# Two layers of a hybrid attention backbone: one output projection with shared weights, new orders of the work, and the first modulation in blocks of 256 columns

## The chip, the cores and the metric

The kernel runs on one core of one Trainium2 chip. The metric is the device time of one execution in microseconds (us). Times of one instruction are given in nanoseconds (ns).

## The reference

Two layers work on 512 latent tokens and 256 context tokens, all with 1024 features, in float32. Cut to what matters here, a layer is:

```python
shift, scale, gate = split(silu(c) @ w_mod + b_mod)        # once for c, once for c_ctx
h = rms_norm(x, norm_g) * (1 + scale) + shift              # latent and context tokens
p = h @ w_in                                               # 11424 columns: heads, z, g
ya, yb, yc = mla(p), diff(p), swa(p)                       # three attention branches
for r, y in enumerate((ya, yb, yc)):
    term[r] = sigmoid(g[r]) * ((y * silu(z[r])) @ w_branch[r])
x = x + gate * ((term[0] + term[1] + term[2]) @ w_out)     # and the same for ctx in layer 0
```

Keys and values are those of the context and the latent tokens together. Layer 0 also makes the context's new values, layer 1 only the latent ones. At the end stands one more RMS norm.

## The kernel before, in words

All large products run on TensorE (PE) as three matmuls each: an operand is split into a high and a low part in a narrower format, and high x high, high x low and low x high are added in PSUM. A weight item is 128 x 1024 values (0.5 MB). It is loaded into one of two buffers `ws`, split by ScalarE (ACT) into the high part and by VectorE (DVE) into the low part, in tiles `wh`, and taken by the products of L444, as every other product is. So `wh` in a row means weights, `s` the features `h` or heads, `pt` transposed probabilities, `bk` one of four single banks of PSUM and `wd` one of two double ones.

The order of all instructions on all engines is fixed while the program is built. `Plan` (L128) keeps a planned time for each engine; two streams hand it work. `stream_a` (L1008) runs attention units: scores into `wd` (`s_pieces`), a softmax on DVE and ACT, transposes (L914) and products with the values (`tv_pieces`, L904). Between them `t_chain` (L892) copies the transposed tile to its high part on ACT and subtracts it on DVE for the low part. `stream_b` (L1209) runs the dense items in the order of two tables of names: `SEQ` for the projections of the input (`K0` keys, `V` values, `Q0` queries of the windowed branch, and so on) and `BR` for the branch stage. It lets up to `DEPTH` = 2 items be under way. Which stream comes next is decided by the planned times, so that the tables and the planner's costs (`dma_t`, L334, and numbers such as 300.0 in `score`) set the order on the chip.

The program begins with the modulation of layer 0 (`begin`, L1902). Of the 3072 columns of `w_mod`, those for scale and shift are loaded as four pieces of 1024 x 512 (n = 2 and 3 scale, 0 and 1 shift; eight loads of 0.25 MB each, `mod_load`), multiplied by the two conditioning vectors (`mod_mm`, L580), evicted, and turned into columns by four small matmuls (`mod_fin`, L592). Feature f of the eight blocks of 128 features needs the pieces f // 4 and 2 + f // 4. x comes behind the first piece; ACT squares it, DVE normalises it (L665), PE transposes it (L682), ACT or DVE apply scale and shift (L703), and both engines split the result. `start_w` lets the weight items in after n = 1, the last piece. All loads named here are issued by the SP queue, in order.

At the end of a layer `out_entry` multiplies by `w_out` in column pieces: for the four latent tokens' tiles 512 + 256 + 256 columns, and in layer 0 after that 512 + 512 columns for the two context tiles, with weights loaded and split again. Behind the last column piece each tile gets its residual, is stored to `x1d` and normalised in place; `next_h` then transposes it and makes the features of layer 1. In layer 0 `next_h` stands between the latent and the context part.

Of the kernel before, what the change touches and what calls it, by code (L numbers as in the profile page):

```python
# [29 lines left out]
BR = [['z7 z1 z2 g4 z4 z0 z3 g3 z5 z6 g0 b0 g1 b1 g2 b2 b4 g5 b5 b3 g6 b6 g7 b7', 'z7 z5 z0 z1 z6 z2 z3 g0 z4 g1 g2 g3 b3 b1 g4 b2 b0 b4 g5 g6 b5 g7 b6 b7', 'z7 z2 z6 z3 z1 z5 z4 g0 z0 g2 g1 g3 g4 g5 b1 g6 g7 b0 b3 b2 b4 b5 b6 b7'], ['g0 z4 z3 z0 z5 z7 z2 z1 z6 b0 g1 g5 b1 g2 b2 g3 g4 b3 b4 g6 g7 b6 b5 b7', 'z0 z5 z2 z1 g2 z4 z6 z7 g0 g1 z3 b0 g4 b1 g3 b4 g5 b5 b3 g6 b6 b2 g7 b7', 'z1 z4 z0 z2 z5 g0 z7 z6 g2 z3 g1 g5 g3 g4 g6 g7 b1 b2 b3 b4 b5 b0 b6 b7']]  # L30
# [10 lines left out]
START = 1  # L41
# [3 lines left out]
SEQ = ["K0 V Q0 Q1 c0 c1 c2 cn Q2 cr p0 p1 Q3 p2 p3 z20 Q4 K1 z21 Q5 z22 Q6 z23 Q7 v0 k0 q0 z24 k1 q1 v1 k2 q2 l0 l1 ln lr k3 q3 v2 k4 q4 k5 q5 v3 k6 q6 k7 q7 u0 w0 z10 z11 u1 w1 z12 z13 u2 w2 z14 z15 u3 w3",  # L45
       "K0 V Q0 Q1 c0 c1 c2 cn Q2 cr p0 p1 Q3 p2 p3 z20 Q4 K1 z21 Q5 z22 Q6 z23 Q7 v0 k0 q0 z24 k1 q1 v1 k2 q2 l0 l1 ln lr k3 q3 v2 k4 q4 k5 q5 v3 k6 q6 k7 q7 u0 w0 z10 z11 u1 w1 z12 z13 u2 w2 z14 z15 u3 w3"]
# [189 lines left out]
def hybrid_kernel(tc, x_in, c_in, ctx_in, c_ctx, w_mod, b_mod, norm_g, w_in, q_norm, w_uq, kv_norm, w_ukv,  # L236
# [274 lines left out]
    def setup():  # L511
# [7 lines left out]
        n, t = rows_of(sc, (c_in[0], c_ctx), nc.scalar)  # L519
# [62 lines left out]
    def mod_fin(l, n, pm, rel, t):  # L582

        (ev, re), = yield from tmps(1)
        t = yield from act(t, ev, pm, psum=True)
        rel.t = t
        po = {}
        if n < 4:
            def emit():
                po["p"], po["r"] = bk.take()  # L590
                for f in range(4):
# [3 lines left out]
            pv = po["p"][:, 0:8].rearrange("p (f j) -> p j f", j=2)  # L595
            o = l * NCOL
            f0 = (n % 2) * 4
            bm = cols[:, o + COL_B + n * 4:o + COL_B + n * 4 + 4]
            for j in range(2):
                if n < 2:  # L600
                    t = yield from tt(t, modc[:, l, j, 8 + f0:12 + f0], pv[:, j], bm, ALU.add)
                else:
                    a = modc[:, l, j, f0:f0 + 4]
                    t = yield from stt(t, a, pv[:, j], 1.0, bm, ALU.add, ALU.add)
                    t = yield from tt(t, a, a, cols[:, o + COL_G + f0:o + COL_G + f0 + 4], ALU.mult)
# [15 lines left out]
        mod_done[l][n].t = t  # L621

    mod_done = [[When() for _ in range(6)] for _ in range(2)]
# [10 lines left out]
    def mod_now(n, r):  # L634
        o = {}
        for kt in range(8):
            def emit():
                if kt == 0:
                    o["p"], o["r"] = bk.take()
                mod_mm(o["p"], kt, r[kt][0][:, 0:512])  # L640
            t = yield from P.pe(lambda: max(r[kt][1], sil_t.t, bk.gate() if kt == 0 else 0.0), 262.0, emit)
            free(1, t)
        yield from mod_fin(0, n, o["p"], o["r"], t)
# [27 lines left out]
    def make_h(l, H, XN, xdone, lat, fs):  # L671
# [113 lines left out]
    def score(row, kgroups, maps):  # L785
# [9 lines left out]
        P.tick(0.0 if maps == 1 else 300.0)  # L795
# [1106 lines left out]
    def begin():  # L1902
# [54 lines left out]
```

## Time and profile before

| | us |
|---|---|
| median of 3 runs | 2715.02 (2711.09 to 2715.76) |
| the profiled execution | 2711.5 |
| its span, first to last instruction | 2709.7 |
| PE busy | 2632.3 |
| VectorE (DVE) busy | 1615.4 |
| ScalarE (ACT) busy | 1350.7 |
| GpSimd (POOL) busy | 179.3 |

Busy time is the time in which an engine has an instruction under way; matmuls are pipelined, and their ends are modelled. A timeline row begins with the start and the length in us, then engine, line, operation, output and input, the count of merged instructions, and in brackets the idle time before it and what ended that.

### The profile page before, as it was taken

The page shows a single profiled execution, that of the slowest core. Times are in us where ns is not written, and L with a number is a line of the kernel's source. Part 1 is how long each engine was busy: PE and PEld are TensorE (multiplying, and loading weights), DVE is VectorE, ACT ScalarE, POOL GpSimd, SP SyncE. Part 2 cuts the span into 40 slices and gives each one's busy share as a digit, 9 for nine tenths or more (in the row PEclk, how much of TensorE's full clock was granted, in tenths as well). Part 3 has the DMA queues.
Part 4 walks back from the last instruction along what each step waited for, and adds up shares of the span by engine and source line. Part 5 has one row for each costly group of instructions (what it writes and reads, how often), then busy time and mean ns, then how long its engine had stood idle before and what let it go on. Part 6 is the DMA issues. An engine that isn't in the chain of part 4 may idle for free. (4 is left out here: it accounts for less than half of the span.)

```text
span 2709.7 us, 42486 instructions
## 1 busy us (share of the span) xinstructions
PE 2632.3 (97%) x16551; PEld 2291.5 (85%) x16551; DVE 1615.4 (60%) x3010; ACT 1350.7 (50%) x2685; POOL 179.3 (7%) x371
## 2 busy tenths in 40 slices
PE   7999999999999999999999998999999999999998
PEld 5888898888888888888888887898888788888887
DVE  4677887666676652142424577887667676534435
ACT  5676775545665551121222366777546565422333
POOL 2101111111100000000000011111101100000000
PEclk8999999999999999999999999999999999999999
DMA  7133211111132463442322533312111223443433
GB/s 237 47 96 85 66 43 48 53 51 42 49 85 85 140 201 117 121 133 63 103 69 64 186 97 91 85 51 65 55 50 38 72 75 98 122 140 101 131 94 133
DMA packets 332318, 249.55 MB, mean 92 GB/s; under 512 B 24870, under 2 KB 296324, under 8 KB 332116
## 3 DMA queue, kind: packets, MB, share of 16 engines
q1 hardware_dynamic: 331472, 246.50, 31.2%
q8 instruction: 130, 2.13, 0.3%
q0 software_dynamic: 416, 0.30, 0.1%
q14 instruction: 72, 0.59, 0.1%
q10 hardware_dynamic: 228, 0.03, 0.0%
HBM read 211.37 MB, written 35.41 MB: 91 GB/s over the span
## 5 line engine op out<-in xcount | busy, mean ns | idle before, releaser
L444 PE MATMUL wd<-s,wh 128*128 128x512 f32 (+1 forms) x4392 | 852.2, 355 | 2.0 <-DVE s L330 1.5
L444 PEld LDWEIGHTS wd<-s,wh 128*128 128x128 f32 x4392 | 723.7, 189 | 123.1 <-issue 6.7
L444 PE MATMUL bk<-s,wh 128*128 128x512 f32 (+1 forms) x3666 | 763.4, 355 | 8.0 <-DVE s L323 1.8
L444 PEld LDWEIGHTS bk<-s,wh 128*128 128x128 f32 x3666 | 584.2, 190 | 94.9 <-issue 6.8
L323 DVE TENSOR_TENSOR wh<-ws,wh 128x1024 fp32r<-128x1024 f32 (+4 forms) x294 | 324.3, 1108 | 522.5 <-ACT wh L309 520.2
L309 ACT ACTIVATE wh<-ws 128x1024 fp32r<-128x1024 f32 (+4 forms) x294 | 282.9, 967 | 537.7 <-PE wd L444 396.4
L309 ACT ACTIVATE pt<-bk 128x512 fp32r<-128x512 f32 (+3 forms) x604 | 342.2, 583 | 204.8 <-PE bk L914 143.3
L444 PE MATMUL bk<-wh,s 128*128 128x256 f32 (+1 forms) x2400 | 351.3, 300 | 3.9 <-DVE pt L323 3.0
L444 PEld LDWEIGHTS bk<-wh,s 128*128 128x128 f32 x2400 | 319.0, 192 | 19.8 <-DVE pt L323 3.7
L323 DVE TENSOR_TENSOR pt<-bk,pt 128x512 fp32r<-128x512 f32 (+5 forms) x428 | 273.3, 656 | 89.7 <-ACT pt L309 69.8
L444 PE MATMUL bk<-pt,s 128*128 128x256 f32 x1888 | 282.7, 289 | 16.2 <-DVE pt L323 10.6
L444 PEld LDWEIGHTS bk<-pt,s 128*128 128x128 f32 x1888 | 252.5, 192 | 41.0 <-DVE pt L323 19.4
L444 PE MATMUL wd<-s,s 128*128 128x256 f32 (+5 forms) x1872 | 274.3, 332 | 10.2 <-ACT s L309 7.4
L309 ACT ACTIVATE s<-wd,ti 128x768 f32<-128x768 f32 (+1 forms) x240 | 195.3, 817 | 137.7 <-DVE ti L826 79.8
L444 PEld LDWEIGHTS wd<-s,s 64*128 64x128 f32 (+2 forms) x1872 | 210.3, 190 | 38.8 <-ACT s L309 11.9
L914 PE MATMUL bk<-ident,s 128*128 128x128 f32 x1472 | 213.0, 278 | 7.9 <-DVE ti L866 3.0
L914 PEld LDWEIGHTS bk<-ident,s 128*128 128x128 f32 x1472 | 173.3, 143 | 34.5 <-ACT s L309 6.1
L309 ACT ACTIVATE s<-s,ti 128x513 f32<-128x513 f32 (+6 forms) x256 | 183.1, 722 | 26.6 <-DVE ti L862 11.0
L309 ACT ACTIVATE s<-bk 128x256 fp32r<-128x256 f32 (+5 forms) x291 | 113.1, 424 | 77.8 <-PE bk L444 76.5
L826 DVE TENSOR_REDUCE ti<-wd 128x1 f32<-128x768 f32 (+1 forms) x160 | 129.3, 845 | 26.0 <-PE wd L444 25.7
L309 ACT ACTIVATE yo<-bk 128x256 f32<-128x256 f32 (+1 forms) x200 | 72.2, 382 | 141.3 <-PE bk L444 140.1
L862 DVE CUSTOM_DVE_ANT_0 s<-wd,s,sinkt 128x512 f32<-128x512 f32 (+2 forms) x160 | 116.3, 743 | 42.1 <-PE wd L444 41.9
(104 smaller groups left out, 1557.1 us busy)
## 6 DMA issues: line engine op xcount, KB each, us to landing
ws<-in_w_in_dram SPq DMA_DIRECT2D x180, 512.0 KB
ws<-in_w_branch_dram SPq DMA_DIRECT2D x48, 512.0 KB
s<-in_w_mod_dram SPq DMA_DIRECT2D x48, 256.0 KB
s<-in_w_mod_dram SPq DMA_DIRECT2D x32, 384.0 KB
ws<-in_w_out_dram SPq DMA_DIRECT2D x24, 512.0 KB
y<-yo SPq DMA_DIRECT2D x80, 128.0 KB
s<-y SPq DMA_DIRECT2D x24, 384.0 KB
s<-s SPq DMA_DIRECT2D x22, 384.0 KB
```

The source lines that it names most:

```text
L309: lambda: nc.scalar.activation(out=out, in_=in_, func=func, scale=scale, **kw))
L323: t = yield from dve(ready, lambda: nc.vector.tensor_tensor(out=out, in0=a, in1=b, op=op), n)
L444: nc.tensor.matmul(o, lhsT=l, rhs=r, start=first, stop=last)
L826: t = yield from dve(t, lambda: nc.vector.tensor_reduce(out=nmx, in_=p[:, lo:hi], axis=AX.X, op=ALU.max, negate=True), n)
L862: t = yield from dve(t, lambda: nc.vector.tensor_tensor_reduce(out=pt_[:, 0:n], in0=p[:, lo:hi], in1=mk, scale=1.0, scalar=sk, op0=ALU.add ...
L914: nc.tensor.transpose(out=pp[:, j * 256 + ri2 * 128:j * 256 + ri2 * 128 + 128], in_=row["P"][:, c:c + 128], identity=ident)
```

## The change

It has five parts. (1) The first modulation is loaded and multiplied in blocks of 256 columns, (n, j) in the order (2,0), (0,0), (2,1), (0,1), (3,0), (1,0), (3,1), (1,1); a feature waits for its two blocks only; the weight items may be loaded from the block (0,0) on, between the blocks. Up to the planned time 45000 ns three items instead of two may be under way. (2) The conditioning vectors are loaded by SP ahead of all else, not by ACT's queue. (3) Layer 0's output projection takes the six token tiles together with one set of weights in 512 + 256 + 256 columns; the two context tiles use a double bank, and `next_h` stands ahead of the last column piece. (4) All the tables in `SEQ` and `BR` have another order. (5) Some of the planner's costs are other numbers.

```diff
-BR = [['z7 z1 z2 g4 z4 z0 z3 g3 z5 z6 g0 b0 g1 b1 g2 b2 b4 g5 b5 b3 g6 b6 g7 b7', ...
+BR = [["z7 z2 g4 z4 z0 z1 z3 z5 z6 g3 g0 g1 g2 b0 b1 b2 g5 b4 g6 b6 b3 b5 g7 b7",
...
-START = 1
+BEGIN = 45000.0
+PACE = 4000.0
-SEQ = ["K0 V Q0 Q1 c0 c1 c2 cn Q2 cr p0 p1 Q3 p2 p3 z20 Q4 K1 z21 Q5 z22 Q6 z23 Q7 v0 k0 q0 z24 k1 ...
+SEQ = ["K0 Q1 Q0 V c0 c2 cn c1 Q2 cr p3 p0 p1 p2 z20 Q3 Q4 K1 z21 Q5 z22 Q6 Q7 ln v0 z23 q0 z24 k1 ...
...
     def dma_t(nbytes):
-        P.free["Q"] = max(P.free["Q"], P.now) + 620.0
-        t = max(P.free["D"], P.free["Q"] + 650.0) + nbytes / 350.0
+        P.free["Q"] = max(P.free["Q"], P.now) + 520.0
+        t = max(P.free["D"], P.free["Q"] + 650.0) + nbytes / 380.0
...
-        n, t = rows_of(sc, (c_in[0], c_ctx), nc.scalar)
+        n, t = rows_of(sc, (c_in[0], c_ctx), nc.sync)
...
-    def mod_load(n):
-        r = []
-        for kt in range(8):
-            w = slot()
-            t = dma(w[:, 0:512], w_mod[0, kt * 128:(kt + 1) * 128, n * 512:(n + 1) * 512])
-            r.append((w, t))
-        return r
+    def mod_load(l, n, j):
+        W = [slot() for _ in range(3)]
+        t = 0.0
+        for i, w in enumerate(W):
+            k = min(3, 8 - 3 * i)
+            t = max(t, dma(w[:, 0:k * 256].rearrange("p (k c) -> p k c", k=k),
+                           w_mod[l, 384 * i:384 * i + 128 * k, n * 512 + j * 256:n * 512 + j * 256 + 256].rearrange("(k p) c -> p k c", p=128)))
+        return W, t
...
-            ready = lambda: max(at(mod_done[l][f // 4]), at(mod_done[l][2 + f // 4]))
+            ready = lambda: max(at(mod_done[l][n_][f % 4 // 2]) for n_ in (f // 4, 2 + f // 4))
...
-        P.tick(0.0 if maps == 1 else 300.0)
+        P.tick(0.0 if maps == 1 else 385.0)
...
-            while left and (not pend or len(pend) < DEPTH and pend[-1][2] and pend[-1][3] and left[0][5]):
+            while left and (not pend or len(pend) < DEPTH + (P.now < BEGIN) and pend[-1][2] and pend[-1][3] and left[0][5]):
...
-        for c, (a, n) in enumerate([(0, 512), (512, 256), (768, 256)]):
-            out_entry(range(2, 6), 0, c, a, n, not cx)
-        if cx:
-            entry(next_h, need=16)
-            for c, (a, n) in enumerate(wide_):
-                out_entry(range(2), 1, c, a, n, True)
+        toks = (2, 3, 4, 5, 0, 1) if cx else (2, 3, 4, 5)
+        for c, (a, n) in enumerate([(0, 512), (512, 256), (768, 256)]):
+            if c == 2 and cx:
+                entry(next_h, need=16)
+            out_entry(toks, c, a, n)
...
     def begin():
-        W = {2: mod_load(2)}
-        setup1()
-        first_load(range(2, 6))
-        P.spawn(mod_now(2, W[2]))
-        make_group(0, LAY[0].h, xs0, xd0, True)
-        for n in (0, 3, 1):
-            yield room(8)
-            P.spawn(mod_now(n, mod_load(n)))
-            if n == START:
-                start_w.t = 0.0
+        first = True
+        for n, j in ((2, 0), (0, 0), (2, 1), (0, 1), (3, 0), (1, 0), (3, 1), (1, 1)):
+            yield lambda: max(room(3)(), P.free["D"] - PACE)
+            P.spawn(mod_now(n, j, *mod_load(0, n, j)))
+            if first:
+                setup1()
+                first_load(range(2, 6))
+                make_group(0, LAY[0].h, xs0, xd0, True)
+                first = False
+            if n == 0 and j == 0:
+                start_w.t = 0.0
...
```

Counted over the whole program, the lists of instructions differ by this: 48 products with 512 columns fewer and 96 with 256 columns more on PE, 64 modulation matmuls of 256 columns for 32 of 512 in the start, eight weight splits fewer on ACT and DVE each, and 881 loads and stores for 895 on SP.

How the order moves is shown at three places; a line of three dots stands for rows left out. The first is PE's queue in the start (`bk0` to `bk3`, `wd0`, `wd1`: banks; `sil`: the conditioning vectors; `ident`: transposes of x; the first number behind a name is the tile's, the last the allocation's). Before, the last rows ahead of the first product with an input weight are:

```order
L580 MATMUL bk3_69<-s82_297,sil_80 32x512
L580 MATMUL bk3_69<-s83_299,sil_80 32x512
L580 MATMUL bk3_69<-s84_301,sil_80 32x512
L580 MATMUL bk3_69<-s85_303,sil_80 32x512
L592 MATMUL bk1_67<-selt_77,pt105_429 128x2 x4
L444 MATMUL bk2_68<-s19_154,wh106_435 128x512
L444 MATMUL bk2_68<-s20_155,wh106_435 128x512
```

and after the change the first products of three items stand on feature 0 (`s14`, `s15`), with modulation blocks still to come behind them:

```order
L693 MATMUL wd0_70<-ident_72,s13_141 128x128
L450 MATMUL bk2_68<-s14_144,wh68_276 128x512
...
L598 MATMUL bk1_67<-selt_77,pt97_366 128x2 x2
L450 MATMUL bk3_69<-s14_144,wh72_292 128x512
...
L450 MATMUL bk0_66<-s14_144,wh95_363 128x512
...
L450 MATMUL bk2_68<-s16_146,wh68_276 128x512
...
L586 MATMUL bk1_67<-s75_314,sil_80 32x256 x3
```

Each of these products has two more rows, the other passes. All matmuls of the start's modulation stood ahead of the products; now four of the eight blocks stand behind the first of them.

The second place is PE's queue at the boundary of the layers. Before, 24 context products of 512 columns stand ahead of the transposes (L682) of the normalised tokens, and 72 behind their beginning:

```order
L444 MATMUL bk3_69<-wh2488_15550,s2443_15252 128x256
L444 MATMUL bk0_66<-wh2494_15616,s2413_14884 128x512
...
L444 MATMUL bk1_67<-wh2503_15737,s2418_14942 128x512
L682 MATMUL wd1_71<-ident_72,s2448_15314 128x128
...
L682 MATMUL wd0_70<-ident_72,s2448_15314 128x128
...
L444 MATMUL bk0_66<-wh2523_15776,s2428_15066 128x512
...
L444 MATMUL bk1_67<-wh2523_15776,s2428_15066 128x512
```

After, 39 context products of 256 columns stand there, 9 between the transposes, and then the first item of layer 1 (weights as the moving tile, features as the other):

```order
L450 MATMUL bk1_67<-wh2488_15668,s2424_15102 128x256
L450 MATMUL wd0_70<-wh2484_15585,s2388_14679 128x256
...
L693 MATMUL wd1_71<-ident_72,s2444_15350 128x128
...
L450 MATMUL wd0_70<-wh2487_15667,s2434_15226 128x256
...
L693 MATMUL wd0_70<-ident_72,s2445_15351 128x128
...
L450 MATMUL bk3_69<-s2496_15763,wh2512_15782 128x512
L450 MATMUL bk3_69<-s2497_15764,wh2512_15782 128x512
...
L450 MATMUL bk2_68<-wh2524_15974,s2496_15763 128x256
```

The context part has moved ahead of the boundary, and what followed the transposes is now layer 1 itself.

The third place is one unit of the attention in layer 0, about 910 us into the profile of before, again on PE. Before, the products with the first pair of tiles (`pt1962`, `pt1963`) stand right behind the unit's 12 transposes:

```order
L914 MATMUL bk0_66<-ident_72,s1950_10698 128x128
...
L914 MATMUL bk2_68<-ident_72,s1950_10698 128x128
...
L914 MATMUL bk3_69<-ident_72,s1950_10698 128x128
L444 MATMUL bk0_66<-pt1962_10756,s1839_10105 128x256
L444 MATMUL bk0_66<-pt1963_10762,s1839_10105 128x256
```

After, 12 products of a dense item stand between (three of them are shown):

```order
L925 MATMUL bk2_68<-ident_72,s1953_10774 128x128
L450 MATMUL bk0_66<-wh1898_10491,s1178_6314 128x256
L450 MATMUL bk0_66<-wh1898_10491,s1179_6315 128x256
L450 MATMUL bk0_66<-wh1899_10492,s1178_6314 128x256
...
L450 MATMUL bk1_67<-pt1965_10835,s1865_10283 128x256
L450 MATMUL bk1_67<-pt1966_10841,s1865_10283 128x256
```

The dense item has moved between the transposes and the products that take them.

## Rows read from the trace of the kernel before

**Rows 1.** The profile page, span and busy time of PE:

```profile
span 2709.7 us, 42486 instructions
...
PE 2632.3 (97%) x16551; PEld 2291.5 (85%) x16551; DVE 1615.4 (60%) x3010; ACT 1350.7 (50%) x2685; POOL 179.3 (7%) x371
```

**Rows 2.** PE by stretches: us, PE busy (instructions), granted clock, DMA share, GB/s:

```profile
0.00:50.00 50.00, 35.24 (x161) 0.86 0.92 302
1500.00:1550.00 50.00, 46.30 (x299) 1.00 0.50 168
1550.00:2350.00 800.00, 776.29 (x5072) 0.99 0.27 75
50.00:950.00 900.00, 876.05 (x6093) 0.99 0.24 69
```

**Rows 3.** PE's waits: who waited for whom, us in total, times, longest:

```profile
PE bk L444 <- DVE pt L323: 15.2, 27, 2.5
PE wd L444 <- ACT s L309: 7.9, 5, 2.6
...
PE bk L444 <- ACT pt L309: 3.3, 5, 1.3
```

**Rows 4.** All engines by stretches: PE, weight load, DVE, ACT, POOL, clock, DMA:

```profile
15.00:20.00 5.00, 3.30 (x9) 0.90 (x10) 3.10 (x13) 3.88 (x20) 1.63 (x4) 0.50 1.04 390
20.00:25.00 5.00, 5.00 (x32) 2.46 (x32) 0.88 (x2) 0.04 (x1) 4.87 (x9) 0.83 1.05 386
...
40.00:50.00 10.00, 8.05 (x30) 5.83 (x30) 7.59 (x20) 8.21 (x25) 2.77 (x2) 0.72 0.70 208
900.00:950.00 50.00, 48.18 (x355) 40.13 (x354) 28.32 (x50) 24.40 (x53) 0.00 (x0) 1.00 0.64 190
```

**Rows 5.** Timeline of PE in the start:

```profile
38.79 1.22 PE L444 MATMUL bk<-s,wh 128*128 128x512 f32 x2 [0.18 <-ACT wh L309]
...
51.60 1.91 PE L682 MATMUL wd<-ident,s 128*128 128x128 f32 x16
...
59.58 12.76 PE L444 MATMUL bk<-wh,s 128*128 128x256 f32 x105
```

**Rows 6.** PE by stretches, products of L444 alone, up to 51.5 us:

```profile
38.70:51.50 12.80, 10.57 (x36) 0.73 0.65 202
```

**Rows 7.** Timeline of PE at the boundary of the layers:

```profile
1545.24 0.49 PE L682 MATMUL wd<-ident,s 128*128 128x128 f32 x3
1549.43 1.64 PE L682 MATMUL wd<-ident,s 128*128 128x128 f32 x13 [3.70 <-DVE s L665]
...
1554.65 14.57 PE L444 MATMUL bk<-wh,s 128*128 128x512 f32 x63
```

**Rows 8.** Timelines of DVE and ACT at the boundary:

```profile
1548.89 1.05 DVE L665 TENSOR_SCALAR s<-s,ti 128x512 f32<-128x512 f32 x2 [3.46 <-DMA x1d<-s]
...
1555.05 0.81 DVE L703 TENSOR_SCALAR pt<-wd,modc 128x512 f32<-128x512 f32 x1
...
1558.87 1.90 DVE L323 TENSOR_TENSOR s<-pt,s 128x512 fp32r<-128x512 f32 x3
...
1551.11 2.17 ACT L309 ACTIVATE pt<-wd,modc 128x512 f32<-128x512 f32 x3 [1.81 <-PE wd L682]
...
1560.71 0.63 ACT L309 ACTIVATE s<-pt 128x512 fp32r<-128x512 f32 x1
```

**Rows 9.** Groups by shape on DVE and ACT: busy us, mean ns:

```profile
L323 DVE TENSOR_TENSOR wh<-ws,wh 128x1024 fp32r<-128x1024 f32 x250 | 305.8, 1223 | 519.6 <-ACT wh L309 517.3 <-DMA s<-x1d 1.5 <-PE bk L914 0.3
L323 DVE TENSOR_TENSOR pt<-bk,pt 128x512 fp32r<-128x512 f32 x352 | 236.5, 686 | 71.0 <-ACT pt L309 68.9
...
L309 ACT ACTIVATE pt<-bk 128x512 fp32r<-128x512 f32 x352 | 202.3, 597 | 151.0 <-PE bk L914 142.2 <-issue 2.6 <-DVE ti L330 1.8
```

**Rows 10.** Timeline of PE in one attention unit of layer 0:

```profile
910.51 1.48 PE L914 MATMUL bk<-ident,s 128*128 128x128 f32 x12
913.14 1.70 PE L444 MATMUL bk<-pt,s 128*128 128x256 f32 x12 [1.16 <-DVE pt L323]
```

More of the change, by code (lines that the diff above doesn't have):

```diff
@@ L590, in emit @@
                 po["p"], po["r"] = bk.take()
-                for f in range(4):
+                for f in range(nf):
                     nc.tensor.matmul(po["p"][:, 2 * f:2 * f + 2], lhsT=ev[:, f * 128:(f + 1) * 128], rhs=selt, start=True, stop=True)
@@ L620, in mod_fin, with mod_all, mod_now, emit @@
         re.t = t
[L621 to L643 removed]
+        for i in range(c0 // 256, (c0 + w) // 256):
+            mod_done[l][n][i].t = t
+    mod_done = [[[When(), When()] for _ in range(6)] for _ in range(2)]
+    def mod_load(l, n, j):
[6 more added lines that the diff above has]
+        return W, t
+    def mod_all(W, pm, c):
+        for k in range(8):
+            mod_mm(pm, k, W[k // 3][:, k % 3 * 256:k % 3 * 256 + 256], c)
+    def mod_now(n, j, W, tw):
+        o = {}
+        def emit():
+            o["p"], o["r"] = bk.take()
+            mod_all(W, o["p"], 0)
+        t = yield from P.pe(lambda: max(tw, sil_t.t, bk.gate()), 1200.0, emit)
+        free(3)
+        yield from mod_fin(0, n, o["p"], o["r"], t, 256 * j, 256)
     def square(t, x, s):
@@ L1622, in h @@
             def h():
[L1623 to L1628 removed]
+                W, t = mod_load(ll, n, j)
                 def chain():
@@ L1633, in emit @@
                             pm[n] = bk.take()
-                        for k in range(8):
-                            mod_mm(pm[n][0], k, W[k // 3][:, k % 3 * 256:k % 3 * 256 + 256], 256 * j)
-                    te = yield from P.pe(lambda: max(t, bk.gate() if j == 0 else 0.0), 750.0, emit)
+                        mod_all(W, pm[n][0], 256 * j)
+                    te = yield from P.pe(lambda: max(t, bk.gate() if j == 0 else 0.0), 1200.0, emit)
                     free(3)
@@ L1786, in chain @@
                         t = max(t, dma(X[tk][h][:, 0:512], src[:, h * 512:(h + 1) * 512]))
-                G[j] = yield from tmps(2)
-                for h in range(2):
-                    t = max(t, dma(G[j][h][0], gate_d[l][j, h * 512:(h + 1) * 512].partition_broadcast(128)))
+                for j in js:
+                    G[j] = yield from tmps(2)
+                    for h in range(2):
+                        t = max(t, dma(G[j][h][0], gate_d[l][j, h * 512:(h + 1) * 512].partition_broadcast(128)))
                 if l == 1:
@@ L1797, in load_res, with out_entry @@
             yield
-        o.rest = [When(), When()]
-        def out_entry(toks, j, c, a0, n, last):
+        o.rest = When()
+        def out_entry(toks, c, a0, n):
             kn = 1024 // n
@@ L1805, in out_entry @@
             steps = [(tk, k) for i in range(8 // kn) for tk in toks for k in range(kn * i, kn * i + kn)]
-            if final and j == 0:
+            if final:
                 steps = [(tk, k) for tk in toks for k in range(8)]
             def release():
-                yield o.rest[j]
-                for _, rg in G[j]:
-                    rg.t = P.now + 3000.0
+                yield o.rest
+                for g in G.values():
+                    for _, rg in g:
+                        rg.t = P.now + 3000.0
             def o_h(*its):
@@ L1861, in o_h @@
                     P.spawn(release())
-                    if last:
-                        free(16, P.now)
+                    free(16, P.now)
             entry(o_h, its)
```

57 lines of the change are left out of this document (26 added, 31 removed), and 5 rows, old and new, of the table BR.

## The prediction

> **What bounds the kernel now.** I read the page first: TensorE (PE) is busy for 2632.3 of 2709.7 us [rows 1], so the change can win only from the 77 us in which PE has nothing to do, or lose by adding to them. Next, PE by stretches says where they lie [rows 2]: 14.8 us in the first 50 us, 24.0 us between 50 and 950 and 23.7 us between 1550 and 2350, which are the attention stages of the two layers, and 3.7 us at 1500 to 1550, the boundary between the layers; most of the rest stands behind the last matmul. Third, PE's waits say what ends the idle time: most of all a product with the transposed probabilities that waits for VectorE's half of their split, 15.2 us in 27 waits, and for ScalarE's, 3.3 us; then scores that wait for a bank of PSUM, 7.9 us [rows 3]. Last come the first 50 us and the boundary instruction by instruction [rows 4 to 8]. The execution took 2711.5 us, its span 2709.7 us; the median of the three runs is 2715.0 us.
>
> **The start: -7 us.** Before, the first product with an input weight is at 38.79 us, behind all eight megabytes of modulation weights; it goes in pieces, and PE is dense only from about 53 us, after the context's transposes at 51.60 us [rows 5]. By 51.5 us PE has issued 36 such products [rows 6], 24 with 512 columns and 12 with 256. A dense product costs 14.57 us / 63 = 0.23 us with 512 columns [rows 7] and 12.76 us / 105 = 0.12 us with 256 [rows 5], so this is 24 x 0.227 + 12 x 0.12 = 6.9 us of work.
>
> After, two features at a time become usable: blocks (2,0) and (0,0) give features 0 and 1, and the order puts three weight items behind each other on every pair. What limits them is the DMA. With the last block, the queue has to bring 8 MB of blocks, 2 MB of x, 1 MB of context and five weight items of 0.5 MB, 13.5 MB or 14.2e6 bytes. The queues moved 386 GB/s where they carried rows of 2 KB, and 190 GB/s at a share of 0.64, so 297 GB/s at a full share, where they carried rows of 1 KB and 0.5 KB [rows 4]; the new blocks have rows of 1 KB. The bounds are therefore 37 and 48 us, plus 2.6 us until it runs (an estimate); I take 340 GB/s, between the two, which gives 44 us. By then features 0 to 5 are on their way; by about 52 us the three items have 3 x 6 x 3 = 54 products behind them, 54 x 0.227 = 12.3 us, and the context's 16 transposes (1.9 us, which before start only at 51.6 us [rows 5]). Gain: 12.3 + 1.9 - 6.9 - 0.3 = 7 us. The fast end of the DMA makes it 11 us, the slow end makes it nothing, since then the last two features are as late as now.
>
> The rest of the start costs nothing. The conditioning vectors go ahead on SP's queue: two issues more there, two fewer on ScalarE's; the first modulation comes earlier, but the path there is x, whose squares keep ScalarE at 3.88 of 5 us in 15 to 20 us [rows 4]. Twice as many modulation matmuls of half the width, four evictions and 16 small VectorE instructions more stand in waits for the same DMA. If that cover went they would be some 4 us.
>
> **The output projection: +0.6 us on PE.** Shared weights remove eight items of 0.5 MB: eight splits on VectorE (1223 ns [rows 9]) and eight on ScalarE, some 10 us of each, and eight SP issues; all of that lies beside PE, which is full while the projection runs, so it is worth nothing. PE's work is not less: 48 products with 512 columns go (48 x 0.227 = 10.9 us), 96 with 256 come (96 x 0.12 = 11.5 us).
>
> **The boundary: +4 us.** Here the change removes cover. Now 24 context products of 512 columns (5.5 us) stand between the last latent product and the transposes for layer 1; the last tokens' residual, norm and store of x1, for which VectorE waits 3.46 us [rows 8], take longer, and PE waits 3.70 us [rows 7]. After, 39 products of 256 columns stand there, 39 x 0.12 = 4.7 us: the wait becomes 4.5 us. Behind the transposes, 63 context products (14.57 us [rows 7]) run now while ScalarE and VectorE make the eight features, 10.2 us from 1551.11 to 1561.34 us [rows 8]. After, nine short ones are left (1.1 us). The first items of layer 1 take up each feature as it comes: 24 products of the key item (5.4 us), 12 short ones of the value item (1.4 us) and 32 transposes (1.91 / 16 = 0.12 us each [rows 5], 3.8 us), with the nine 11.8 us. VectorE meanwhile has two weight splits (2.4 us), three modulations (0.81 us), eight feature splits (1.90 / 3 = 0.63 us) [rows 8, 9] and some 4 us of small work for the context's tokens, 14 us until the context's transposes can follow: PE waits some 3 us in pieces. Sum: 0.8 + 3, say 4 us. The bounds are 0 (the weight splits come out of the features' way) and +12 us (no product of layer 1 fits between).
>
> **The orders: -12 us.** For each pair of probability tiles I counted in the order what PE issues between its transposes and the first product on it, priced as above: in 65 of the 384 pairs it is under 1.8 us before, in 36 after; under 1.0 us in 25 and 12. The chain that has to fit is a ScalarE copy (597 ns), a VectorE subtraction (686 ns) [rows 9] and the hand-overs. One such place shows it: 12 transposes, then the products at once and 1.16 us of wait [rows 10]; after, 12 other products stand between. I take half of 15.2 + 3.3 us as gone, -9, and a tenth of the other 29 us of the two stages, -3, because the count from scores to their transposes is hardly better. Bounds: -30, which leaves the other 18 of the 48 us, and +20, a new wait for nearly each that goes.
>
> **The sum.** 2711.5 - 7 + 0.6 + 4 - 12 = 2697.1 us. The median of the runs lies 3.5 us above the profiled execution; I add half of it and say **2699 us**, 0.6% below the median. The branch stages (1000 to 1500, and from 2350) and the tail stay: PE is full there, and layer 1's output projection is the same.
>
> **The rivals.** (a) *The waits only move.* PE takes its instructions in order, and what is pulled ahead of one wait is missing at the next. Against it speaks the count; for it, that VectorE and ScalarE need the same time as before. Orders 0: 2711.5 - 7 + 0.6 + 4 = 2709.1, about 2711 us on the median: no change. (b) *The new order makes more waits than it removes, slower.* The place is PE in the two attention stages, before scores that need a bank and before transposes, which my count does not price. The two stages wait 47.7 us now; 20 us more is 2711 + 20 = 2731 us. It decides from the point where the orders cost more than 4 us (2711 + 4 = 2715), and shows as slower from 10 us. (c) *The clock stays low at the start.* The granted clock was 0.50 in 15 to 20 us and 0.72 in 40 to 50 us [rows 4], where PE worked in short pieces; the early products come in such pieces. At 1.2 GHz a product takes twice 0.23 us; the 18 products and 16 transposes behind 42 us then need some 12 us for 10, and the start gains 3 instead of 7: 2703 us. The Trainium skill ("TensorE: Matmul & The Clock Gate", section "HAM oscillation — how this bites in real kernels") says that products in bursts between waits for DMA let the clock fall again and again, and speaks against this part of the change; before's stretches agree at 0.50 and 0.72, while 20 to 25 us, equally fed by DMA, had 0.83. (d) *The start does not come.* SP's queue is in order, and the third weight item waits there for VectorE's split of the first; if that is late, the blocks behind it are late, and the start gains nothing: 2706 us. (e) *The orders remove 30 us*: 2681 us.
>
> **How the numbers follow.** My forecast 0.50, (a) 0.14, (b) 0.11, (c) 0.10, (d) 0.05, (e) 0.10. About 0.2%, 5.4 us, is what a measurement can tell from no change: faster is below 2709.6 us. That holds for nearly all of the forecast, for (c), (e) and most of (d): 0.72; (a) and the upper edge of the forecast make 0.17; (b) is 0.11. The range leaves out (b) and half of (e): 2682 to 2715 us.
>
> **What would show it.** In the profile after: the first product with an input weight near 26 us, features 6 and 7 near 50 us, PE dense from there; at the boundary two waits, about 4.5 us before the transposes and some 3 us in pieces behind them; the waits of products for the split near 9 us. A third weight item issued much later than 22 us on SP would show (d); a granted clock of 0.5 at 40 to 50 us shows (c); waits of scores for banks well above 8 us show (b), and more than 60 us of idle time in the two attention stages makes the forecast wrong.

## The result and the profile after

The changed kernel takes **2695.69 us** (median of 4 runs, 2695.27 to 2696.05) against 2713.89 us for the kernel before on the same chip (4 runs, 2711.09 to 2715.76): ratio 0.9934, 95% interval [0.9917, 0.9951], which is 17.9 us less. Ratios and intervals below are to the kernel before on the same chip; since the chips differ, kernels are compared by their ratios. Two single executions, of 10648 us (setup_sp) and 3194 us (pool_late_sink_last), were slow ones and are left out of every figure. The forecast was 2699 us, range 2682 to 2715, faster. The total came as forecast; of its terms the start had the wrong sign, the orders were too small by nearly half, and the boundary with the output projection was too large. The profiled execution took 2695.27 us.

The page of the changed kernel, which answers to [rows 1]:

```profile
span 2693.5 us, 42670 instructions
...
PE 2627.3 (98%) x16663; PEld 2288.1 (85%) x16663; DVE 1609.1 (60%) x3017; ACT 1347.5 (50%) x2686; POOL 170.3 (6%) x371
```

PE's idle time is 66.2 us where it was 77.4, and its busy time is 5.0 us shorter although it has 112 instructions more. The same stretches as in [rows 2], changed kernel:

```profile
0.00:50.00 50.00, 32.18 (x202) 0.98 0.99 301
1500.00:1550.00 50.00, 48.70 (x301) 1.00 0.28 82
1550.00:2350.00 800.00, 784.76 (x5178) 0.99 0.27 76
50.00:950.00 900.00, 878.75 (x6124) 0.99 0.25 69
```

PE is less busy in the first 50 us, not more; most of what was won lies in the attention stages, above all in layer 1's (8.5 us less idle). PE's waits in the changed kernel, which answer to [rows 3]:

```profile
PE bk L450 <- DVE pt L329: 10.1, 18, 2.7
...
PE bk L586 <- DVE modc L329: 5.0, 1, 5.0
PE bk L925 <- DVE s L814: 4.4, 1, 4.4
...
PE wd L450 <- ACT s L315: 1.9, 4, 0.5
...
PE bk L450 <- ACT pt L315: 0.9, 2, 0.5
```

Products that waited for VectorE's split went from 15.2 to 10.1 us, those for ScalarE's from 3.3 to 0.9, and products that wait for a wide bank of scores from 7.9 to 1.9. Two single waits are new: 5.0 us for modulation columns (`modc`) and 4.4 us for a row of probabilities.

The 5.0 us stand in the start. Timeline of PE there, changed kernel:

```profile
28.03 0.95 PE L450 MATMUL bk<-s,wh 128*128 128x512 f32 x3
...
42.84 0.94 PE L450 MATMUL bk<-s,wh 128*128 128x512 f32 x3
48.77 1.93 PE L586 MATMUL bk<-s,sil 128*32 128x256 f32 x16 [4.99 <-DVE modc L329]
...
62.06 8.26 PE L450 MATMUL bk<-s,wh 128*128 128x512 f32 x40 [1.13 <-DVE s L329]
```

The first product came 10.8 us earlier than before [rows 5], but PE is dense only from 62 us. Followed back, engine by engine; ScalarE, then VectorE, then POOL of the same execution:

```profile
48.69 0.78 ACT L315 ACTIVATE pt<-wd,modc 128x512 f32<-128x512 f32 x1 [7.20 <-DVE modc L329]
```

```profile
47.70 0.88 DVE L676 TENSOR_SCALAR s<-s,ti 128x512 f32<-128x512 f32 x2 [8.53 <-POOL ti L669]
48.50 0.22 DVE L329 TENSOR_TENSOR modc<-bk,cols 128x2 f32<-128x2 f32 x2
```

```profile
37.38 0.55 POOL L669 TENSOR_TENSOR ti<-ti,mhalf 128x1 f32<-128x1 f32 x1 [20.93 <-DVE modc L336]
37.99 0.75 POOL L347 DMA_DIRECT2D s<-in_mla_q_norm_dram  x1
...
46.53 0.54 POOL L347 DMA_DIRECT2D sinkt<-in_swa_sink_dram  x1
47.09 0.58 POOL L669 TENSOR_TENSOR ti<-ti,mhalf 128x1 f32<-128x1 f32 x1
```

POOL computes the power that turns a token's mean square into its norm. Between the powers of the two context tokens stand thirteen small loads of `setup2`, which keep POOL's queue for 9.1 us, from 37.99 to 47.09. VectorE waits 8.53 us for the second power, and behind it in VectorE's order stand the modulation columns, for which ScalarE and, through a bank of PSUM, PE wait. Before, the same loads stood on POOL between 20.4 and 28.9 us, with both context powers behind them at 43.95 and 46.25 us, so that no power waited for them; the new `begin` issues context and `setup2` close together.

### The profile page after: what moved, and what is told of

It reads as the page before. It is cut to its first block, busy times and chain, and to the rows that moved or that the text cites. A ratio compares the mean times of both kernels' runs of the same rounds, so it can differ in the third digit from the quotient of the medians.

```text
span 2693.5 us, 42670 instructions
## 1 busy us (share of the span) xinstructions
PE 2627.3 (98%) x16663; PEld 2288.1 (85%) x16663; DVE 1609.1 (60%) x3017; ACT 1347.5 (50%) x2686; POOL 170.3 (6%) x371
## 5 line engine op out<-in xcount | busy, mean ns | idle before, releaser
L450 PE MATMUL bk<-s,wh 128*128 128x512 f32 (+1 forms) x3666 | 780.1, 358 | 11.4 <-DVE pt L329 6.7
L329 DVE TENSOR_TENSOR wh<-ws,wh 128x1024 fp32r<-128x1024 f32 (+4 forms) x286 | 315.5, 1108 | 540.3 <-ACT wh L315 533.1
L315 ACT ACTIVATE wh<-ws 128x1024 fp32r<-128x1024 f32 (+4 forms) x286 | 274.4, 964 | 559.3 <-PE wd L450 401.7
L450 PE MATMUL bk<-wh,s 128*128 128x256 f32 (+1 forms) x2304 | 323.1, 294 | 1.7 <-DVE pt L329 0.6
L329 DVE TENSOR_TENSOR pt<-bk,pt 128x512 fp32r<-128x512 f32 (+4 forms) x424 | 270.8, 655 | 84.1 <-ACT pt L315 65.6
L450 PEld LDWEIGHTS bk<-wh,s 128*128 128x128 f32 x2304 | 297.7, 191 | 13.6 <-issue 1.8
L450 PE MATMUL bk<-pt,s 128*128 128x256 f32 x1888 | 275.9, 286 | 4.9 <-DVE pt L329 2.8
L315 ACT ACTIVATE s<-s,ti 128x513 f32<-128x513 f32 (+6 forms) x260 | 186.3, 723 | 30.7 <-DVE ti L873 12.4
L315 ACT ACTIVATE s<-bk 128x256 fp32r<-128x256 f32 (+7 forms) x291 | 112.9, 424 | 58.0 <-PE bk L450 56.8
```

The lines of the kernel that those rows point to most:

```text
L315: lambda: nc.scalar.activation(out=out, in_=in_, func=func, scale=scale, **kw))
L329: t = yield from dve(ready, lambda: nc.vector.tensor_tensor(out=out, in0=a, in1=b, op=op), n)
L450: nc.tensor.matmul(o, lhsT=l, rhs=r, start=first, stop=last)
```

## Experiments on the start

All kernels below compute the whole reference. A gauge for the start is the work of products with an input weight in the first 75 us: their count by shape, priced as in the prediction at 0.227 us for 512 columns and 0.12 us for 256 (an estimate; the rows of two kernels are shown).

| kernel | x512, x256 | work by 75 us | ratio to before |
|---|---|---|---|
| before | 37, 168 | 28.6 us | 1 |
| changed | 72, 53 | 22.7 us | 0.9934 |
| setup_sp | 72, 68 | 24.5 us | 0.9929 |
| pool_late | 72, 84 | 26.4 us | 0.9921 |
| pool_late_sink_last | 72, 94 | 27.6 us | 0.9919 |
| ctx_loads_last | 72, 94 | 27.6 us | 0.9927 |
| after_old_start | 72, 127 | 31.6 us | 0.9912 |
| old_start_vectors_first | 72, 120 | 30.7 us | 0.9929 |

The ratios of neighbouring rows have overlapping intervals; the order of the whole is clearer than any one step. The rows of the changed kernel:

```profile
L450 PE MATMUL bk<-s,wh 128*128 128x512 f32 x72 | 20.9, 425 | 2.0 <-DVE s L329 1.1 <-ACT s L315 0.9
...
L450 PE MATMUL bk<-s,wh 128*128 128x256 f32 x53 | 7.4, 297 | 0.7 <-DVE s L329 0.7
```

**pool_late: the thirteen loads behind both powers.** All of `setup2` moves. In `begin`:

```
-        yield room(3)
+        yield lambda: max(room(3)(), at(xd0[0]), at(xd0[1]))
         setup2()
```

> The changed kernel with one edit: the thirteen small loads that setup2 issues from POOL are put behind the two powers of the context tokens on POOL, where they stood between them. The orders of TensorE, ScalarE and SyncE stay as they are. Theory (POOL's queue): the changed kernel loses its start because the second context token's power runs at 47.09 us, behind 9.1 us of issues; then VectorE's wait of 8.53 us, ScalarE's of 7.20 us and TensorE's of 4.99 us near 48 us go together, TensorE is dense from about 57 us where it was 62, and the time is 2690 to 2692 us. Rival (something else is late next: the last blocks' loads, or the splits of h on VectorE and ScalarE): the 4.99 us wait is replaced by others before 62 us, and the time stays at 2694 to 2696 us.

Measured 2691.57 us (5 runs, 2688.56 to 2694.57), ratio 0.9921 [0.9908, 0.9935]: some 3.5 us less than the changed kernel by the ratios, with intervals that overlap; the range of the theory holds it. VectorE and PE in the start of pool_late:

```profile
52.13 0.18 DVE L562 TENSOR_SCALAR sinkt<-sinkt 128x32 f32<-128x32 f32 x1 [3.12 <-DMA sinkt<-in_swa_sink_dram]
```

```profile
46.20 1.32 PE L586 MATMUL bk<-s,sil 128*32 128x256 f32 x16
...
53.79 0.61 PE L598 MATMUL bk<-selt,pt 128*128 128x2 f32 x4 [1.95 <-DVE modc L336]
...
57.92 8.96 PE L450 MATMUL bk<-s,wh 128*128 128x512 f32 x41 [0.84 <-DVE s L329]
```

The wait of 4.99 us is gone and PE is dense 4.1 us earlier, so POOL's queue is shown as the cause of that wait, and so as one cause of the late start. A smaller one took its place: the first VectorE instruction of `setup2`'s chain waits 3.12 us for the last of the small loads and holds the last `modc` behind it.

**setup_sp: the loads issued by SyncE.** The issuing engine of thirteen loads changes, nothing else.

```
...
-        ts = dma(sinkt, sink.rearrange("l h -> (l h)").partition_broadcast(128), nc.gpsimd)
+        ts = dma(sinkt, sink.rearrange("l h -> (l h)").partition_broadcast(128), nc.sync)
...
```

> The changed kernel with one edit: the thirteen small loads of setup2 are issued by SyncE where POOL issued them; the orders of TensorE, VectorE and ScalarE are the same to the last instruction. Theory (POOL's queue): the same gain as with the loads behind both powers, 2690 to 2692 us, if SyncE has room for 13 issues of about half a microsecond before the first layer's weights. Rival (SyncE's queue is the one that is full there): the weights behind them come some 7 us later, TensorE waits for DMA after 55 us, and the time is 2694 to 2700 us.

Measured 2693.18 us (4 runs, 2692.83 to 2695.60), ratio 0.9929 [0.9915, 0.9942], between the ranges of theory and rival. On VectorE the wait for POOL's power shrank to 0.66 us, but the same sink instruction now stood 4.75 us for its load:

```profile
39.63 0.88 DVE L676 TENSOR_SCALAR s<-s,ti 128x512 f32<-128x512 f32 x2 [0.66 <-POOL ti L669]
...
53.74 0.18 DVE L562 TENSOR_SCALAR sinkt<-sinkt 128x32 f32<-128x32 f32 x1 [4.75 <-DMA sinkt<-in_swa_sink_dram]
```

**pool_late_sink_last: besides, the sink instruction at the end of its chain.**

```
...
         def chain():
-            yield from dve(ts, lambda: nc.vector.tensor_scalar(out=sinkt, ...
             tcol = yield from columns(st, n, t, cols[:, 32:32 + n])
...
             free(3)
+            yield from dve(ts, lambda: nc.vector.tensor_scalar(out=sinkt, ...
...
```

> The changed kernel with two edits: the thirteen loads of setup2 behind both context powers on POOL (as in the run before), and the sign change of the sink vector, the first VectorE instruction that waits for those loads, put at the end of setup2's chain. TensorE's order is the same but for the place of one small transpose. Theory (VectorE's queue is the second half of the POOL fault): with the loads late alone, VectorE stood 3.12 us at 52.13 us for the sink vector's load, ahead of the last modulation columns, and TensorE 1.95 us for these; both waits go, TensorE is dense from about 55 us, and the time is 2687.5 to 2690 us. Rival (the splits of h or the last modulation block are as late): another wait of the same size before 60 us, and 2691 to 2693 us.

Measured 2691.23 us (4 runs, 2687.54 to 2692.81), ratio 0.9919 [0.9905, 0.9932]: the rival, and not to be told from pool_late. Both waits went, PE is dense at 57.27 us, 0.65 us earlier; a product waits 1.88 us at 56.15 us for ScalarE's split of the next feature instead. So with these two waits gone, features 6 and 7 are still late.

**ctx_loads_last: besides, the context rows loaded behind all eight blocks.** The four lines that load the context move from behind block (3,0) to the end of `begin`.

> As the kernel with loads late and sink last, and besides the context rows are loaded behind all eight modulation blocks, as in the kernel before, where the changed kernel loads them ahead of the last two. Theory (the start is bound by the bytes that stand ahead of the last modulation block): 1 MB less ahead of it, so the last block's matmuls come about 3 us earlier than 46.2 us and features 6 and 7 with them, while the context products come later; 2686 to 2689 us. Rival (the context columns are wanted as early as features 6 and 7): TensorE waits for them instead, and 2690 to 2695 us.

Measured 2693.28 us (5 runs, 2689.36 to 2695.47), ratio 0.9927 [0.9914, 0.9941]: the rival again. The last block's matmuls came at 44.02 us instead of 46.87 in pool_late_sink_last, but ScalarE, in order, stood 3.64 us for the context's rows until 44.74 us and squared them ahead of the split that PE wanted: PE waited 1.93 us for it, and 1.72 us for a bank with the context's transposes:

```profile
47.02 0.49 PE L450 MATMUL bk<-s,wh 128*128 128x512 f32 x1 [1.93 <-ACT s L315]
```

The work by 75 us is the same.

**after_old_start: the changed kernel with the whole start of the kernel before.** `begin`, `mod_load` and `mod_now` of before, conditioning vectors on ScalarE's queue, no third open entry.

> The changed kernel with the start of the kernel before (modulation blocks of 512 columns, conditioning vectors on ScalarE's queue, two open entries), the new tables, costs and output projection kept. Theory (the new start lost 5 to 6 us where 7 were forecast to be won): 2689 to 2692 us, with as many columns of products in the first 75 us as the kernel before. Rival (the tables were made for the new start and lose elsewhere what the old start wins): 2694 to 2702 us, with the difference behind 75 us. If the new start won 7 us as forecast: 2702 us or more with the loss in the first 75 us.

Measured **2689.04 us** (4 runs, 2686.61 to 2691.34), ratio 0.9912 [0.9899, 0.9926]: the theory, and the lowest median of the study, below both kernels. PE in its start, and its products:

```profile
34.21 1.90 PE L585 MATMUL bk<-s,sil 128*32 128x512 f32 x4 [0.81 <-DMA s<-in_w_mod_dram]
...
37.81 0.73 PE L449 MATMUL bk<-s,wh 128*128 128x512 f32 x2
...
50.21 8.88 PE L449 MATMUL bk<-s,wh 128*128 128x512 f32 x60
```

```profile
L449 PE MATMUL bk<-s,wh 128*128 128x512 f32 x72 | 18.5, 402 | 2.0 <-DVE s L328 1.1 <-DVE wh L328 0.7 <-ACT s L314 0.2
...
L449 PE MATMUL bk<-s,wh 128*128 128x256 f32 x72 | 9.2, 284 | 0.0
...
L449 PE MATMUL bk<-wh,s 128*128 128x256 f32 x55 | 6.8, 283 | 0.0
```

The first product is 9.8 us later than in the changed kernel and PE is dense 11.9 us earlier; the last modulation piece is through at 36.1 us, where the changed kernel's last block is through at 50.7. By the ratios the new start costs 0.22%, 6 us. The two intervals overlap a little, but the next run gives the same 6 us clear of no change.

**before_new_start: the new start alone on the kernel before.**

> The kernel before with the new start alone (blocks of 256 columns, conditioning vectors on SyncE, a third open entry in the first 45 us), with the old tables, costs and output projection. In its POOL queue both context powers stand ahead of the thirteen small loads. Theory (the new start is worth what was forecast, and POOL's queue ate it in the changed kernel): TensorE is dense about 7 us earlier than in the kernel before, no wait for modc over 2 us, and 2704 to 2710 us. Rival (the new start is worth nothing by itself: smaller blocks bring the first product forward but the eighth feature comes no earlier): busy time of TensorE in the first 75 us at or under the 60.24 us of the kernel before, and 2712 to 2720 us.

Measured 2718.72 us, ratio 1.0022 [1.0012, 1.0033]: slower by 6 us, the rival. PE in the first 75 us, kernel before and before_new_start:

```profile
0.00:75.00 75.00, 60.24 (x352) 0.91 0.67 217
```

```profile
0.00:75.00 75.00, 54.11 (x372) 0.93 0.71 216
```

The products are 24 with 512 columns and 137 with 256, 21.9 us of work against 28.6. This kernel has both powers ahead of the small loads on POOL, so POOL is not the only cause.

**old_start_vectors_first: of the new start only the conditioning vectors, put back into after_old_start.**

```
-        n, t = rows_of(sc, (c_in[0], c_ctx), nc.scalar)
+        n, t = rows_of(sc, (c_in[0], c_ctx), nc.sync)
```

> The changed kernel with the old start, as in the run after_old_start, and one part of the new start put back: the two conditioning vectors are issued by SyncE ahead of the first modulation block; the orders of TensorE, VectorE and POOL are the same. Theory (the loss sits in the blocks of 256 columns and what is loaded between them; the vectors by themselves help little, since x's rows and their norms decide when the first transposes can run): the wait for c falls from 4.5 to about 2.9 us, the first modulation product is 2 to 3 us earlier, the transposes of x stay near 21 us, and the time stays within 1 us of after_old_start, 2688 to 2690 us. Rival (the vectors are what the old start lacked): the transposes of x come 2 us earlier and so does all behind them, 2686 to 2687.5 us. Other rival (two issues more ahead of the blocks on SyncE hold everything back): 2690 to 2692 us.

Measured 2692.95 us (6 runs, 2686.75 to 2700.84), ratio 0.9929 [0.9914, 0.9944]; the median lies in none of the three ranges, and the interval overlaps after_old_start's, so no gain, perhaps a loss. By the gauge it is 0.9 us of work. The wait for `c` fell to 2.90 us, the first modulation matmuls came at 7.38 instead of 7.61 us, and the transposes of x at 22.36 instead of 21.04: the vectors' wait was replaced by one of 4.23 us for `sil`.

## Experiments on the orders and the output projection

**after_old_orders: old tables and old planner's costs in the changed kernel.**

> The changed kernel with the tables SEQ and BR and the planner's costs of the kernel before; the new start and the shared output projection stay. If the new orders brought 23 to 25 us, as the comparison of the two traces suggests, and the start and the layer boundary cost about 3 us each: 2716 to 2722 us, with the lost time of TensorE in the attention stretches (75 to 950 us and 1600 to 2350 us). If the orders brought 12 us and the start 7, as forecast: 2705 to 2711 us.

Measured 2716.68 us, ratio 1.0017 [1.0008, 1.0025]: the first case. The orders are worth 1.0017 - 0.9934 = 0.83%, 22.5 us, and the start and the output projection together cost 4.6 us.

**after_old_costs and after_old_tables: only one half of the orders taken back.**

```
-        P.free["Q"] = max(P.free["Q"], P.now) + 520.0
-        t = max(P.free["D"], P.free["Q"] + 650.0) + nbytes / 380.0
+        P.free["Q"] = max(P.free["Q"], P.now) + 620.0
+        t = max(P.free["D"], P.free["Q"] + 650.0) + nbytes / 350.0
...
-        P.tick(0.0 if maps == 1 else 385.0)
+        P.tick(0.0 if maps == 1 else 300.0)
...
-                    te = yield from P.pe(lambda: max(t, bk.gate() if j == 0 else 0.0), 1200.0, emit)
+                    te = yield from P.pe(lambda: max(t, bk.gate() if j == 0 else 0.0), 750.0, emit)
```

That is the edit of after_old_costs; after_old_tables puts the old `SEQ` and `BR` back instead.

> The changed kernel with the planner's costs of the kernel before (DMA issue 620 ns and 350 GB/s where it has 520 and 380, 300 where it has 385 behind the two-map units, 750 where it has 1200 for a modulation block of layer 1), the new tables kept. Theory (the tables SEQ and BR bring the 22 us): 2694 to 2701 us. Rival (the costs bring them): 2708 to 2716 us, with the waits of products for a wide bank back near 8 us in the second layer's attention.

> The changed kernel with the tables SEQ and BR of the kernel before, the new costs kept. Theory (the tables bring the 22 us): 2711 to 2718 us, with TensorE's waits in both attention stages at those of the kernel with all old orders. Rival (the costs bring them): 2697 to 2704 us. Half and half, each fitted to the other: both this kernel and the one with the old costs lie at 2703 to 2712 us.

Measured 2713.18 us, ratio 1.0002 [0.9994, 1.0011], with the old costs, and 2717.18 us, 1.0024 [1.0013, 1.0034], with the old tables. Each time lies in the range of the case that gives the whole gain to the half taken back, the costs in one run and the tables in the other. Both cannot be true, so neither account holds, and half and half does not either: each half alone brings next to nothing. Against after_old_orders the new tables alone win 0.15% and the new costs alone lose 0.07%, hardly more than the noise; together they win 0.83%. PE in layer 1's attention, 1600 to 2350 us, in the kernel before, the changed kernel, and with old costs, old tables and old orders (one fence each):

```profile
1600.00:2350.00 750.00, 726.29 (x4752) 0.99 0.26 73
```

```profile
1600.00:2350.00 750.00, 737.51 (x4827) 1.00 0.27 75
```

```profile
1600.00:2350.00 750.00, 729.22 (x4785) 0.99 0.26 73
```

```profile
1600.00:2350.00 750.00, 726.27 (x4784) 0.99 0.27 73
```

```profile
1600.00:2350.00 750.00, 727.44 (x4765) 0.99 0.26 72
```

Idle there: 23.7, 12.5, 20.8, 23.7 and 22.6 us. With the old costs the products' wait for a wide bank, 7.9 us there before, is down to 0.5 us, and yet the time stays: other waits have come in its place, 4.2 us for VectorE's split of features or heads (1.1 in the changed kernel) the largest of them. The tables say which step comes next, the costs at which modelled time the planner thinks an engine is free; the order that PE gets comes out of both, so a table stands only with the costs it goes with.

**before_new_orders: tables and costs together on the kernel before.**

> The kernel before with the new tables SEQ and BR and the new planner's costs together; its start and its output projection stay. The tables alone and the costs alone brought nothing, both together about 22 us, in the changed kernel. Theory (tables and costs belong together, the start and the output projection are apart from them): 2688 to 2694 us, with TensorE's waits in both attention stages as low as in the changed kernel, and the boundary's 3 us saved besides. Rival (the tables fit only the very program that they were made with, so a shifted start or boundary throws them off as other costs did): 2700 to 2714 us, with the loss behind the layer boundary, where the plan differs from the changed kernel's.

Measured 2692.65 us (5 runs, 2687.58 to 2694.89), ratio 0.9925 [0.9911, 0.9938]: the theory, -0.75% or 20.4 us. Layer 1's attention, 1600 to 2350 us, has 737.36 us of busy time as in the changed kernel. Other costs threw the tables off, another start and another output projection did not. The boundary's wait, though, is not saved; PE stands 5.3 us there for the last tokens' norm, longer than before [rows 7]:

```profile
PE wd L687 <- DVE s L670: 5.3, 1, 5.3
```

**before_new_out: the shared output projection alone on the kernel before.** The hunks on `load_res`, `out_entry` and their entries.

> The kernel before with the new output projection alone (all six tokens from one reading of the weights, next_h ahead of the third column group). Forecast of the boundary: 4 us of waits and 0.6 us more matmuls, so 2716 to 2719 us, with the waits between 1545 and 1575 us. Rival (the boundary is covered as before and the projection costs nothing): 2711 to 2714 us. Everything behind the boundary is planned anew with the old tables, so a part of the difference may lie in the second layer's attention; the stretch 1500 to 1600 us is what counts.

Measured 2714.47 us, ratio 1.0006 [0.9997, 1.0015]: +1.6 us, from -0.8 to +4, just outside the rival's range and below the forecast's. PE waits 3.3 us between 1530 and 1600 us where it waited 3.7. With the new orders the same part can be read from two runs above: before_new_orders and after_old_start differ in nothing but the output projection, and there it wins 0.13%, 3.5 us, with overlapping intervals. Its sign is not settled.

## Why the prediction was right, and where not

**The orders, forecast -12, measured -20 to -22.5 us.** The mechanism was right, the term mis-sized. First, the count of pairs priced only the waits of products for the split: they fell by 5.1 + 2.4 = 7.5 us, near the 9 taken. The scores' waits for a wide bank [rows 3] were put into "a tenth of the other 29 us", 3 us; they alone gave 6.0. Second, a wait was priced at its own length, and some cost more. PE in the kernel before around two of the bank waits, then the stretches from the end of each:

```profile
2137.42 1.85 PE L444 MATMUL wd<-s,s 64*128 64x256 f32 x11 [1.44 <-ACT s L309]
...
2180.52 1.32 PE L444 MATMUL wd<-s,s 96*128 96x256 f32 x6 [2.43 <-ACT s L309]
```

```profile
2138.00:2142.00 4.00, 4.00 (x22) 0.58 0.36 92
...
2182.00:2186.00 4.00, 3.95 (x18) 0.57 0.25 69
```

In the 4 us right behind each of the two waits the mean granted clock is 0.58 and 0.57, so that PE, though it was full, worked there for some 3 us at the lower level of 1.2 GHz. In the changed kernel 2138 to 2142 us have no such wait and a clock of 1.00. Not every wait had that price: before, the 3.70 us at the boundary [rows 7] and the 1.78 us ahead of 249.34 us were followed by 4 us at 1.00, and so was one of 2.69 us ahead of 1690.89 us in the changed kernel. What decides it stays open. Over the whole span the granted clock is 0.993 against 0.990, and that difference is 0.003 x 2700 = 8 us at most (an estimate; some 3 us of it are in the first 75 us, 0.95 against 0.91), beside some 17 us less idle time in 75 to 950 and 1600 to 2350 us (24.0 to 18.5 and 23.7 to 12.5). One of the changed kernel's four runs also has 0.990, at 2696.05 us, so the mean clock by itself does not set the time. In layer 0 a new wait of 4.4 us stands near 204 us, behind a weight split for which VectorE stood 5.43 us; from 204 to 209 us the clock is 0.53 as well. Rivals (a) and (b), waits that only move or multiply, did not come: the two attention stages of [rows 2] are idle for 36.5 us where it was 47.7; but after_old_tables and after_old_costs show that the new costs, or the new tables, alone would have made (a) true.

**The start, forecast -7, measured +6 us.** Two steps of this term failed. "The rest of the start costs nothing" was costed for SyncE, ScalarE and PE and never for POOL: that `setup2`'s thirteen issues now stand between the context's two powers was not looked at. That is some 3.5 us, which pool_late takes back. The second is "by about 52 us the three items have 54 products", and that PE is dense from there. The rate of the DMA was right (338 GB/s from 20 to 30 us, where 340 was taken), the arrival nearly: in pool_late the last block's matmuls run at 46.20 us, the forecast said 44. Through 51.84 us this kernel has 51 of the 54 products. But from the last block to dense work it took not 8 but 11.7 us, to 57.92, through the transposed columns, `modc`, the modulation and the splits of two features for latent and context tokens on two engines that also work for the others. With the old start the distance is longer, 16.0 us from 34.21 to 50.21, but PE has 36 products to do in it and it begins 12 us earlier. The product count by 51.5 us was the wrong gauge: it counted what comes forward and not the end of the bytes, from which all eight features follow. Which share of the last 4.0 us of work (27.6 against 31.6 us) belongs to the later last block and which to ScalarE and VectorE stays open; the context's megabyte alone is not it, and the clock is not needed for it: ctx_loads_last has a granted clock of 1.00 over the first 75 us and the same 27.6 us.

Rival (c) came in part, but it does not explain the loss. In pool_late PE worked in pieces between waits from 52 to 58 us; 55 to 60 us of pool_late and of after_old_start:

```profile
55.00:60.00 5.00, 3.26 (x8) 0.54 0.00 0
```

```profile
55.00:60.00 5.00, 4.11 (x36) 1.00 0.02 3
```

In the changed kernel itself the low stretches were 45 to 55 us (0.82 and 0.84 in steps of 5 us) and 60 to 65 us (0.69); of 40 to 50 us, where (c) looked for 0.5, the first half had 1.00. But the old start has such a stretch too: the kernel before had 0.50 from 40 to 45 us, and its mean over the first 75 us is the lower one, 0.91 against

```profile
0.00:75.00 75.00, 54.46 (x336) 0.95 0.67 203
```

in the changed kernel. The rule cited there (the Trainium skill, "TensorE: Matmul & The Clock Gate", section "HAM oscillation — how this bites in real kernels") spoke against this part of the change; pool_late's row agrees in kind, though the waits of that stretch were for VectorE and ScalarE and not for DMA (share 0.00). Rival (d), a third weight item late on SyncE, did not come: it is issued at 21.13 us.

**The boundary, forecast +4, and the output projection, +0.6: measured +1.6 us together on the kernel before, -0.8 to +4, and -3.5 us with the new orders.** The waits were placed wrong. PE at the boundary, changed kernel:

```profile
1562.62 2.06 PE L450 MATMUL wd<-wh,s 128*128 128x256 f32 x12 [2.38 <-DVE pt L329]
1564.47 1.91 PE L693 MATMUL wd<-ident,s 128*128 128x128 f32 x8
...
1568.16 1.97 PE L693 MATMUL wd<-ident,s 128*128 128x128 f32 x16 [0.32 <-DVE pt L714]
```

There is no wait of 4.5 us before the transposes; PE waits 2.38 us for a wide bank that VectorE has not yet read, ahead of the last products of the projection, so that the norm is done when they end. Behind the transposes only 0.32 us of the forecast 3 came: layer 1's products of features fit between. Over 1500 to 1600 us the waits are 4.0 us, before 3.7 [rows 7].

**The sum.** -22.5 + 6 + 1.6 is -15 us from single parts, -17.9 measured, within the intervals of the parts. The forecast's -14.4 came near the total because the start's error of 13 us and the orders' of 8 to 10, with 3 or more from the boundary, nearly cancelled. That the total came out is luck in this sense. In the prediction's working three things are off besides: the 0.3 us taken from the start's gain has no source; rival (c) makes 12 us out of 10, which costs 2 us and not the 4 it takes; and the slow bound of the DMA, 297 GB/s, is not that of 1 KB rows (last section). Only the first stands in the sum.

## What to carry to other kernels

When a change moves a step, list its instructions on every queue, small loads on a compute engine's queue too, and look for the latency-bound instruction that they now stand in front of; then look at the first consumer of those loads on its own in-order engine. In a start that is full of DMA, count back from the last byte that everything needs and not from the first product that comes forward. In this kernel a table of orders and the costs of its planner were one object: take both or neither.

## What the runs showed of the hardware

At full load, transfers with shorter rows moved fewer bytes. The DMA queues from 20 to 30 us: first the kernel before, whose modulation pieces have rows of 2 KB, then the changed kernel, whose blocks have rows of 1 KB and whose weight items, under way at the same time, mostly rows of 0.5 KB:

```profile
DMA packets 2355, 3.84 MB, mean 384 GB/s; under 512 B 464, under 2 KB 494, under 8 KB 2354
...
q1 hardware_dynamic: 2098, 3.81, 103.5%
```

```profile
DMA packets 3942, 3.38 MB, mean 338 GB/s; under 512 B 135, under 2 KB 3941, under 8 KB 3941
...
q1 hardware_dynamic: 3941, 3.37, 110.7%
```

All engines are full in both, and the mix of shorter rows, 855 bytes per packet against 1816 on the main queue, brings 12% fewer bytes. The two sizes can be told apart within the changed kernel: from 22 to 23 us, with rows of 1 KB (357 packets, 0.35 MB), the queues moved 348 GB/s; from 16 to 19 us, with mostly 0.5 KB (1640 packets, 0.89 MB), 296 GB/s. The Trainium skill ("DMA: Bandwidth & Descriptors", section "Specifications") gives 512 B as the transfer from which the line rate is reached; these stretches differ from it, and the measurement decides.

And on PE several waits of some 2.5 us, single or two close together, were followed by some 3 us at half the clock, so the price of such a wait was up to twice its length (an estimate); others as long, and one of 3.70 us, were not.
